# More load buffers for the experts, and another order of the last sums and the last norm, in a fused three-layer block on one core

## The chip, the cores and the metric

The program runs on one core of a Trainium2 chip. The metric is the device time of one execution in microseconds (us); a kernel's time is the median of several runs. Five engines work side by side, each on its own queue in order: TensorE (PE in the profile; its weight loads are PEld), VectorE (DVE), ScalarE (ACT), GpSimd (POOL, unused here) and SyncE (SP), which issues all the DMAs.

## The reference

A first block (three kinds of attention and a SwiGLU) is followed by a second one of two layers; each layer has a mixer and a feed-forward part, each closed by a layer norm. Sequence 256, width 1024, all in float32. The change concerns the last part only, the mixture of experts of the last layer and the layer norm behind it:

```python
def moe_swiglu(h, w_router, w_gate, w_up, w_down):          # 8 experts, 2 per token, width 3584 each
    hf = h.reshape(t, d)
    logits = (hf @ w_router).astype(jnp.float32)
    top_val, top_idx = lax.top_k(logits, TOP_K)
    gates = jax.nn.softmax(top_val, axis=-1)
    ...
    def expert_block(args):
        xb, e = args
        return (jax.nn.silu(xb @ w_gate[e]) * (xb @ w_up[e])) @ w_down[e]
    ...
    out = jnp.einsum('tk,tkd->td', gates.astype(y.dtype), y)

h = layer_norm(DEEPNORM_ALPHA * h + y, ln_g[layer, 1], ln_b[layer, 1])   # eps 1e-5; this is the output
```

## The kernel before

All weights come from DRAM as one stream of tiles of 128 x 2048 float32 (1 MB each), in an order fixed at build time: 142 tiles for what stands ahead of the experts and 42 for each of the eight experts, 478 in all. The class `Stream` keeps that order. It has a first-in, first-out list `free` of buffers ("slots"), and `fill` issues the next load on SP whenever a slot is on the list and the tile's address is known (`base`). SP's queue is in order too: a load whose slot is still being read holds back the loads behind it.

A tile is used in one of two ways. For most matmuls it is first split: ScalarE copies it to a rounded high part `wh` (L307), VectorE subtracts to get the low part `wl` (L309), in two pieces each; `mm3` (L482 to L491) then runs three matmuls for each product, first all that use `wh`, then those that use `wl`. `begin` gives the slot back to `free` behind the split. The parts lie in two rings of four buffers each in the pool `wp` (`HI` and `LO`), and `get` keeps as many tiles split ahead as the ring is long. Or a tile is used whole, in float32 (`get_whole`), and its slot is free when TensorE has read it.

In the experts the slots are two of `wp` (`RAW`), three of `wx`, three of `wx2`, one of `wx3` and one of `wln`, ten together. Besides, `spare`, a tile of the pool `act` under the tag `xl` (two buffers), is lent for one load (`W.lend`, L1707). When that load has been split, the buffer goes to `yy`, the scaled output of a heavy expert; the tag's other buffer holds `macc`, the sum over the experts.

The experts are ordered by how many tokens they got. Experts 0, 2, 4, 6 in this order are "heavy" (`expert`, 128 slots, split weights), 1, 3, 5, 7 are "light" (`expert_few`, 64 slots, whole weights). Each goes through steps c: matmuls of gate and up (`gu`), Silu (ACT) times up (`sg`, DVE), transposes (`uT`), the copy of their result (`uf` or `uh`, ACT), and the matmuls with the down weights (`dn`) of the step before. `turns` deals out steps of heavy and light experts in turn, by hand; in bursts of mostly six tiles. The whole section `experts` is issued in program order on all engines (`manual_schedule(engines=ALL)`). The routing (`gates`, `in_order`) runs inside step 1 of the first heavy expert; `in_order` ends with SP reading the addresses of the experts 1 to 7 (L1367). In step 3 `begin_few` gathers the inputs of all light experts (`few` by DVE, `gx` by PE, `xfew` by ACT).

An expert's output is scaled by its gate (L1486 for a heavy one, `ye` L1622 for a light one) and scattered back to the tokens by matmuls into PSUM (`scatter`, tiles `sp`), and DVE adds that to `macc` (L1456). The scatter of an expert is run later, within a following step (the list `late`). The last light expert does it in another way: in its step 7, ahead of the `dn` matmuls, `macc` is put into four PSUM banks by matmuls with the identity (`sum`, L1611), the scatter adds to these banks, DVE takes statistics from them (L1630) and ACT copies them back to `macc` (L1631).

Then `normed` does the layer norm: mean and variance (L1686), the root by `inv_sqrt` on DVE alone (a first guess by integer shifts and three Newton steps, between them the four subtractions `centred`, L1690, which read `macc`), the four scalings (L1697), and a DMA of each result to the output. Behind it stands `If(most > 0)`: the function `again`, for tokens beyond an expert's room, which runs only if an expert overflowed, and `normed` once more.

Of the kernel before, what the change touches and what calls it, by code (L numbers as in the profile page):

```python
# [216 lines left out]
class Stream:  # L217
# [3 lines left out]
    def __init__(self, nc, src, items, raw, hi, lo):  # L221
# [4 lines left out]
        self.slots, self.free, self.holds, self.count = [], [], {}, {}  # L226
# [10 lines left out]
    def room(self, pools):  # L237

        new = []
        for p in pools:  # L240
            k = self.count[p] = self.count.get(p, 0) + 1
            new.append((p, f"wr{k}"))
        self.slots += new
        self.free = new + self.free

    def _part(self, kind):
        ring = self.rings[kind]
        p = ring[self.turn[kind] % len(ring)]
        self.turn[kind] += 1
        return p.tile([128, 2048], F32R, tag="w" + kind, name="w" + kind, bufs=ring.count(p))  # L250
# [18 lines left out]

    def spare(self):  # L270

        p, tag = self.free.pop(0)
        return p.tile([128, 2048], F32, tag=tag, name="wr", bufs=1)

    def load(self, n):

        while self.n_load < n:
# [4 lines left out]
            self._load(slot[0].tile([128, 2048], F32, tag=slot[1], name="wr", bufs=1))  # L282
# [6 lines left out]
    def lend(self, t):  # L289

        self._load(t)

    def _taken(self, i):
        if i in self.home:
            self.free.append(self.home.pop(i))
# [55 lines left out]
def tile_kernel(ctx: ExitStack, tc: tile.TileContext, cst, par, wst, x, mem, g_mix, g_mem, g_ffn, w_forget,  # L351
# [87 lines left out]

    def inv_sqrt(m, eps, between):  # L440


        v, r, w = (mo.tile([128, 2], F32, name=n) for n in ("iv", "ir", "iw"))
        i = mo.tile([128, 2], I32, name="ii")
        V.tensor_scalar(out=v, in0=m, scalar1=eps, scalar2=None, op0=ALU.add)
        V.tensor_scalar(out=i, in0=v.bitcast(I32), scalar1=1, scalar2=None, op0=ALU.logical_shift_right)
        V.tensor_scalar(out=i, in0=i, scalar1=-1.0, scalar2=float(0x5f3759df), op0=ALU.mult, op1=ALU.add)
        r0 = i.bitcast(F32)
        for step in range(4):
            between[step]()  # L450
            if step == 3:
                return r
            V.tensor_tensor(w, r0, r0, op=ALU.mult)
            V.scalar_tensor_tensor(out=w, in0=w, scalar=-0.5, in1=v, op0=ALU.mult, op1=ALU.mult)
            V.scalar_tensor_tensor(out=r, in0=w, scalar=1.5, in1=r0, op0=ALU.add, op1=ALU.mult)
            r0 = r
# [930 lines left out]
    def hidden(pg, pu):  # L1387

        sg = sm.tile([128, 512], F32, name="sg", tag="sq", bufs=2)[:, 0:pg.shape[-1]]
        A.activation(out=sg, in_=pg, func=AF.Silu)  # L1390
        V.tensor_tensor(sg, sg, pu, op=ALU.mult)
# [40 lines left out]
    spare = act.tile([128, 2048], F32, name="wr", tag="xl")  # L1432
    macc = act.tile([128, 2, D], F32, name="macc", tag="xl")
    yy = act.tile([128, 2, D], F32R, name="yy", tag="xl")
# [25 lines left out]
    def expert(Pm, s, after, late, begun=None, last=False):  # L1460
# [20 lines left out]
        y = (yy[:, 0], yy[:, 1])  # L1481
# [8 lines left out]
        def scatter(t):  # L1490
            for n in range(2):
# [4 lines left out]
                added(t, n, ps, last)  # L1496

        ws = widths(s)
        for c in range(len(ws) + 1):
# [29 lines left out]
            if c == 4 and after is not None:  # L1529
                Pn = slots(rkp[:, :, after], 0)  # L1530
            if c:
# [36 lines left out]
    def expert_few(s, late, last=False):  # L1568
# [15 lines left out]
        for c in range(8):  # L1584
            end = c == 7
            if not end:
# [12 lines left out]
                turn = hidden(ps[:, 0], ps[:, 1])  # L1599
# [6 lines left out]
            if end and last:  # L1606

                for t in range(2):
                    for n in range(2):
                        summed.append(pa("sum"))  # L1610
# [13 lines left out]
        def scatter(t):  # L1624
# [12 lines left out]
    left = {}  # L1637
# [45 lines left out]
    def normed():  # L1683
# [3 lines left out]

        def centred(t, c):
            cc = slice(c * 512, c * 512 + 512)
            return lambda: V.scalar_tensor_tensor(out=done[:, t, cc], in0=macc[:, t, cc], scalar=mv[:, t, 0:1],  # L1690
                                                  in1=gbf[:, cc], op0=ALU.subtract, op1=ALU.mult)

        r = inv_sqrt(mv[:, :, 1], 1e-5, [centred(t, c) for t in range(2) for c in range(2)])
# [78 lines left out]
```

## Time and profile before

| what | us |
|---|---|
| median of 3 runs (1851.49 to 1852.97) | 1852.12 |
| the profiled execution | 1851.57 |
| its span, first to last instruction | 1849.3 |
| TensorE busy (share of the span) | 1809.3 (98%) |
| VectorE busy | 1107.7 (60%) |
| ScalarE busy | 874.0 (47%) |

The profile is one execution; the span leaves out 2.3 us before the first and behind the last instruction. Shares of busy time are means over stages with different limits; matmuls are pipelined and their ends modelled, so a busy TensorE need not be at its peak. "Idle before" an instruction is what its engine stood still, and the name behind the arrow is what ended it. The DMA share is the mean busy share of the core's 16 DMA engines; it can read slightly above 1.

### The profile page before, as it was taken

How to read it: one execution, taken by the hardware profiler on the slowest of the kernel's cores; microseconds unless marked ns; L12 is line 12 of the kernel's file. 1: busy time of each engine (PE TensorE's matmuls, PEld its weight loads, DVE VectorE, ACT ScalarE, POOL GpSimd, SP SyncE). 2: the span in 40 equal slices, each digit the busy share in tenths (PEclk: the TensorE clock that was granted, in tenths of full speed). 3: DMA queues.
4: the chain of work that ended last, by engine and by line, in shares of the span. 5: the costliest groups of instructions: out<-in, count | busy, mean ns of one | idle time of the engine just before them, and what ended most of it. 6: DMA issues, size and time to landing. Idle time of an engine off the chain costs nothing.

```text
span 1849.3 us, 27608 instructions
## 1 busy us (share of the span) xinstructions
PE 1809.3 (98%) x11150; PEld 1443.3 (78%) x11150; DVE 1107.7 (60%) x1609; ACT 874.0 (47%) x1224; POOL 0.2 (0%) x4
## 2 busy tenths in 40 slices
PE   8999999999999999999999999999999999999996
PEld 7888898999899899987787767766777676766662
DVE  7756556554577765467779654664656554654522
ACT  6655565444433354435546444553444444553520
POOL 0000000000000000000000000000000000000000
PEclk9999999999999999999999999999999999999998
DMA  7534344655443555544356799999999999999995
GB/s 263 180 117 157 115 160 171 221 189 203 146 159 135 201 198 195 200 165 159 117 227 237 285 389 420 419 419 420 419 419 419 419 419 420 419 419 419 410 419 220
DMA packets 73287, 512.70 MB, mean 277 GB/s; under 512 B 8512, under 2 KB 9152, under 8 KB 12096
## 3 DMA queue, kind: packets, MB, share of 16 engines
q1 hardware_dynamic: 73152, 510.86, 69.9%
q8 instruction: 89, 1.46, 0.3%
q14 instruction: 46, 0.38, 0.1%
HBM read 509.78 MB, written 1.05 MB: 276 GB/s over the span
## 4 chain that ended last, share of the span: by engine, by line
PE 83%; DMA 9%; DVE 6%; ACT 1%; issue 1%; SPq 0%; DVEq 0%; ACTq 0%
DMA wr<-in_wst_dram 8%; PE gu L1593 8%; PE fm L482 7%; PE fm L493 7%; PE fm L486 7%; PE gu L482 5%; PE gu L484 5%; PE gu L491 5%; PE dn L1617 4%; DVE wl L309 3%; PE tk L482 3%; PE tk L484 3%; PE acc L484 3%; PE tk L491 3%; PE acc L482 3%; PE acc L491 3%
## 5 line engine op out<-in xcount | busy, mean ns | idle before, releaser
L309 DVE TENSOR_TENSOR wl<-wr,wh 128x1024 fp32r<-128x1024 f32 x620 | 729.7, 1219 | 355.4 <-ACT wh L307 340.5
L307 ACT ACTIVATE wh<-wr 128x1024 fp32r<-128x1024 f32 x620 | 617.6, 1051 | 297.6 <-issue 84.4
L482 PE MATMUL fm<-xh,wh 128*128 128x256 f32 x1056 | 251.2, 280 | 0.0
L486 PE MATMUL fm<-xl,wh 128*128 128x256 f32 x1056 | 249.4, 278 | 0.0
L1593 PE MATMUL gu<-wr,xfew 128*64 128x256 f32 x1792 | 207.9, 385 | 0.0
L482 PEld LDWEIGHTS fm<-xh,wh 128*128 128x128 f32 x1056 | 198.8, 188 | 1.1 <-issue 0.2
L486 PEld LDWEIGHTS fm<-xl,wh 128*128 128x128 f32 x1056 | 198.6, 188 | 0.9
L1593 PEld LDWEIGHTS gu<-wr,xfew 128*64 128x64 f32 x1792 | 124.8, 138 | 77.4 <-issue 21.1
L482 PE MATMUL gu<-wh,xe 128*128 128x512 f32 (+1 forms) x448 | 177.7, 398 | 0.0
L484 PE MATMUL gu<-wh,xe 128*128 128x512 f32 (+1 forms) x448 | 173.0, 388 | 0.0
L493 PE MATMUL fm<-xh,wl 128*128 128x256 f32 x1056 | 145.4, 278 | 0.0
L493 PEld LDWEIGHTS fm<-xh,wl 128*128 128x128 f32 x1056 | 131.5, 188 | 0.0
L491 PE MATMUL gu<-wl,xe 128*128 128x512 f32 (+1 forms) x448 | 119.3, 388 | 0.4 <-DVE wl L309 0.4
L482 PE MATMUL tk<-wh,xh 128*128 128x512 f32 x288 | 116.6, 405 | 1.7 <-ACT wh L307 1.5
L484 PE MATMUL tk<-wh,xl 128*128 128x512 f32 x288 | 114.5, 397 | 0.4 <-DVE xl L464 0.4
L482 PEld LDWEIGHTS gu<-wh,xe 128*128 128x128 f32 x448 | 84.2, 188 | 31.6 <-ACT wh L307 13.0
L1581 ACT ACTIVATE uf<-uT 128x256 f32<-128x256 f32 x28 | 10.8, 384 | 204.6 <-PE uT L1579 204.6
L1617 PE MATMUL dn<-wr,uf 128*64 128x512 f32 x448 | 103.1, 594 | 2.8 <-ACT uf L1581 1.4
L491 PEld LDWEIGHTS gu<-wl,xe 128*128 128x128 f32 x448 | 83.0, 188 | 19.0 <-DVE wl L309 1.1
L484 PEld LDWEIGHTS gu<-wh,xe 128*128 128x128 f32 x448 | 84.2, 188 | 16.5 <-DVE xe L464 0.3
L482 PE MATMUL dn<-wh,uh 128*128 128x512 f32 x224 | 89.2, 398 | 0.0
L484 PE MATMUL dn<-wh,ul 128*128 128x512 f32 x224 | 88.0, 393 | 0.0
(348 smaller groups left out, 2281.9 us busy)
## 6 DMA issues: line engine op xcount, KB each, us to landing
wr<-in_wst_dram SPq DMA_DIRECT2D x477, 1024.0 KB, 11.8
gb<-in_ln_g_dram SPq DMA_DIRECT2D x3, 512.0 KB, 5.7
gb<-in_ln_b_dram SPq DMA_DIRECT2D x3, 512.0 KB, 6.5
memt<-in_mem_dram SPq DMA_DIRECT2D x2, 512.0 KB, 6.9
res<-in_x_dram SPq DMA_DIRECT2D x2, 512.0 KB, 12.7
wr<-in_wst_dram SPq DMA_DIRECT2D x4, 256.0 KB, 15.6
out_dram<-wr SPq DMA_DIRECT2D x4, 256.0 KB, 3.1
gb<-in_g_mem_dram SPq DMA_DIRECT2D x1, 512.0 KB, 5.3
```

The source lines that it names most:

```text
L307: self.nc.scalar.activation(out=h[:, c], in_=t[:, c], func=AF.Copy)
L309: return [lambda c=c: self.nc.vector.tensor_tensor(l[:, c], t[:, c], h[:, c].bitcast(F32), op=ALU.subtract) for c in cols]
L482: T.matmul(ps, ah, bh, start=first and i == 0, stop=False)
L484: T.matmul(ps, al, bh, start=False, stop=False)
L486: T.matmul(ps, ah, bl, start=False, stop=False)
L491: T.matmul(ps, ah, bl, start=False, stop=last and i == n - 1)
L493: T.matmul(ps, al, bh, start=False, stop=last and i == n - 1)
L1581: A.activation(out=U, in_=pT, func=AF.Copy)
L1593: T.matmul(ps[h, g], xfew[:, u + k, i * FEW:i * FEW + FEW], w[:, k, 256 * b:256 * b + 256], start=u + k == 0, stop=u + k == KD - 1)
L1617: T.matmul(acc[h], U[:, j, b * FEW:b * FEW + FEW], wd[n][:, k], start=c == 1 and k == 0, stop=end and k == 3)
```

## The change

1. **Slots.** `spare`'s buffer is no longer lent for one load but put at the head of `free` for good. `fewer_parts`, called as the experts begin, shortens each ring of parts from four to three and appends one slot of the tag `wh` and one of `wl` to `free`; the tags keep four buffers each, which parts and loads then share.
2. **`yy`** has no buffer of its own any more. In the last step but one of a heavy expert `keep` marks that the next slot that comes free is held back; in its last step `borrow` makes `yy` in it, and `give`, behind the second scatter's matmuls, puts the slot on `free`.
3. **The last sums.** The identity matmuls of `sum` move from step 7 to step 6 of the last light expert, ahead of that step's `dn`; one of the four banks comes from the other PSUM pool. `normed` reads the sums from PSUM; the copies to `macc` come behind it.
4. **The last root.** `inv_sqrt` is replaced by Ln and Exp on ScalarE with one Newton step on DVE behind the subtractions. Behind the last Silu ScalarE loads the table with Ln and Exp.

```diff
+    def fewer_parts(self):
+        for kind in "hl":
+            ring = self.rings[kind]
+            self.free.append((ring[0], "w" + kind, len(ring)))
+            self.deep[kind] = len(ring)
+            ring.pop()
...
-        return p.tile([128, 2048], F32R, tag="w" + kind, name="w" + kind, bufs=ring.count(p))
+        return p.tile([128, 2048], F32R, tag="w" + kind, name="w" + kind, bufs=self.deep.get(kind, ring.count(p)))
...
+    def keep(self):
+        self.wanted = True
+
+    def borrow(self, name):
+        slot, self.kept = self.kept, None
+        return self._new(slot, F32R, name), lambda: self.free.append(slot)
...
     def _taken(self, i):
         if i in self.home:
-            self.free.append(self.home.pop(i))
+            slot = self.home.pop(i)
+            if self.wanted:
+                self.wanted, self.kept = False, slot
+            else:
+                self.free.append(slot)
...
-    def hidden(pg, pu):
+    def hidden(pg, pu, final=False):
...
         A.activation(out=sg, in_=pg, func=AF.Silu)
+        if final:
+            A.preload_act_table_set(LOGEXP)
...
-    spare = act.tile([128, 2048], F32, name="wr", tag="xl")
     macc = act.tile([128, 2, D], F32, name="macc", tag="xl")
-    yy = act.tile([128, 2, D], F32R, name="yy", tag="xl")
...
-        y = (yy[:, 0], yy[:, 1])
+        y = give = None
...
                 added(t, n, ps, last)
+            if t:
+                give()
...
+            if c == len(ws) - 1:
+                W.keep()
+            if end:
+                yy, give = W.borrow("yy")
+                y = (yy[:, 0:D], yy[:, D:2 * D])
...
-            if end and last:
+            if c == 6 and last:
                 for t in range(2):
                     for n in range(2):
-                        summed.append(pa("sum"))
+                        summed.append((pb if t + n == 0 else pa)("sum"))
                         T.matmul(summed[-1], ident, macc[:, t, n * 512:n * 512 + 512], start=True, stop=False)
...
                 if last:
                     V.bn_stats(out=fst[:, t, n], in_=pss[n])
-                    A.activation(out=macc[:, t, n * 512:n * 512 + 512], in_=pss[n], func=AF.Copy)
+                    sums.append(pss[n])
...
         W.after = True
+        W.fewer_parts()
...
+        V.tensor_scalar(out=v, in0=mv[:, :, 1], scalar1=1e-5, scalar2=None, op0=ALU.add)
+        A.activation(out=r, in_=v, func=AF.Ln)
+        A.activation(out=r, in_=r, func=AF.Exp, scale=-0.5)
+        cols = [(t, slice(n * 512, n * 512 + 512), part(t, n)) for t in range(2) for n in range(2)]
+        for t, cc, ps in cols:
+            V.scalar_tensor_tensor(out=done[:, t, cc], in0=ps, scalar=mv[:, t, 0:1], in1=gbf[:, cc], op0=ALU.subtract,
+                                   op1=ALU.mult)
+        V.tensor_tensor(w, r, r, op=ALU.mult)
+        V.scalar_tensor_tensor(out=w, in0=w, scalar=-0.5, in1=v, op0=ALU.mult, op1=ALU.mult)
+        V.scalar_tensor_tensor(out=r, in0=w, scalar=1.5, in1=r, op0=ALU.add, op1=ALU.mult)
...
-        W.lend(spare)
+        W.free.insert(0, (act, "xl", 2))
...
-        normed()
+        normed(lambda t, n: sums[2 * t + n])
+        for i, ps in enumerate(sums):
+            A.activation(out=macc[:, i // 2, i % 2 * 512:i % 2 * 512 + 512], in_=ps, func=AF.Copy)
```

## Rows read from the trace of the kernel before

**Rows 1.** The page: busy us by engine; DMA share in 40 slices; issues of loads.
```profile
PE 1809.3 (98%) x11150; PEld 1443.3 (78%) x11150; DVE 1107.7 (60%) x1609; ACT 874.0 (47%) x1224; POOL 0.2 (0%) x4
...
DMA  7534344655443555544356799999999999999995
...
wr<-in_wst_dram SPq DMA_DIRECT2D x477, 1024.0 KB, 11.8
```
**Rows 2.** Waits of TensorE from 1062 us on: us in total, times, longest us.
```profile
PE sp L1627 <- DVE macc L1456: 3.1, 2, 2.2
PE dn L1617 <- ACT uf L1581: 1.4, 3, 0.5
PE dn L1617 <- DMA wr<-in_wst_dram: 1.4, 1, 1.4
```
**Rows 3.** Windows: us, busy by engine (PE, PEld, DVE, ACT, POOL), PEclk, DMA share, GB/s.
```profile
995.00:1005.00 10.00, 7.47 (x33) 5.38 (x32) 9.55 (x32) 7.18 (x8) 0.00 (x0) 1.00 0.06 8
1035.00:1045.00 10.00, 10.00 (x50) 8.58 (x50) 3.68 (x5) 6.13 (x9) 0.00 (x0) 1.00 0.23 96
1060.00:1070.00 10.00, 10.00 (x80) 6.82 (x80) 0.00 (x0) 0.16 (x1) 0.00 (x0) 1.00 0.40 138
1070.00:1820.00 750.00, 742.85 (x4277) 516.43 (x4272) 402.77 (x416) 338.07 (x414) 0.00 (x0) 1.00 1.01 419
```
**Rows 4.** Waits of SP, 960 to 1110 us, the largest.
```profile
SPq L266 <- DVE wl L309: 72.8, 28, 12.2
```
**Rows 5.** Timeline near 1685 us: start, us, engine, line, out<-in, count, [idle before, releaser].
```profile
1682.80 2.36 DVE L309 TENSOR_TENSOR wl<-wr,wh 128x1024 fp32r<-128x1024 f32 x2 [13.25 <-ACT wh L307]
...
1685.08 1.27 DVE L1456 TENSOR_TENSOR macc<-macc,sp 128x512 f32<-128x512 f32 x2
1685.81 2.67 PE L1627 MATMUL sp<-ye,PU 64*128 64x512 f32 x4 [2.19 <-DVE macc L1456]
```
**Rows 6.** Window of the stretch at half clock.
```profile
1685.86:1692.68 6.82, 6.82 (x24) 3.36 (x26) 6.82 (x8) 4.35 (x5) 0.00 (x0) 0.50 1.02 420
```
**Rows 7.** Waits of TensorE in the first heavy expert, 985 to 1062 us.
```profile
PE uT L1474 <- DVE sg L1391: 2.1, 1, 2.1
PE gx L1564 <- DVE few L1557: 1.9, 1, 1.9
```
**Rows 8.** Timeline of a heavy burst: fifth and sixth tile split; fourth, fifth used.
```profile
1727.38 4.63 DVE L309 TENSOR_TENSOR wl<-wr,wh 128x1024 fp32r<-128x1024 f32 x4 [0.25 <-ACT wh L307]
...
1732.93 1.08 PE L491 MATMUL gu<-wl,xe 128*128 128x512 f32 x4
...
1735.69 1.09 PE L491 MATMUL dn<-wl,uh 128*128 128x512 f32 x4
```
**Rows 9.** Timeline of TensorE in steps 6 and 7 of the last light expert.
```profile
1817.84 1.04 PE L1617 MATMUL dn<-wr,uf 128*64 128x512 f32 x2
1820.25 3.65 PE L1617 MATMUL dn<-wr,uf 128*64 128x512 f32 x14 [1.37 <-DMA wr<-in_wst_dram]
...
1824.10 3.60 PE L1611 MATMUL sum<-macc,cs 128*128 128x512 f32 x8
1827.63 3.65 PE L1617 MATMUL dn<-wr,uf 128*64 128x512 f32 x16
```
**Rows 10.** Timeline of DVE in the last norm.
```profile
1836.02 0.17 DVE L445 TENSOR_SCALAR iv<-mv 128x2 f32<-128x2 f32 x1
...
1840.26 0.16 DVE L455 SCALAR_TENSOR_TENSOR ir<-iw,ir 128x2 f32<-128x2 f32 x1
...
1841.00 2.73 DVE L1697 SCALAR_TENSOR_TENSOR wr<-wr,ir 128x512 f32<-128x512 f32 x4
```
**Rows 11.** Groups of DVE by line, 950 to 970 us: busy us, mean ns, idle before.
```profile
L977 DVE SCALAR_TENSOR_TENSOR res<-res,nw,gb 128x512 f32<-128x512 f32 x4 | 2.8, 748 | 0.1
...
L966 DVE SCALAR_TENSOR_TENSOR res<-res,acc 128x512 f32<-128x512 f32 x4 | 2.7, 680 | 1.0 <-PE acc L491 1.0
```
**Rows 12.** Timeline of ScalarE in an earlier norm: Ln; Exp takes the same.
```profile
966.32 0.20 ACT L428 ACTIVATE nr<-nv 128x1 f32<-128x1 f32 x1
```

More of the change, by code (lines that the diff above doesn't have):

```diff
@@ L225, in __init__ @@
         self.base = {None: 0}
-        self.slots, self.free, self.holds, self.count = [], [], {}, {}
+        self.free, self.count, self.deep, self.wanted, self.kept = [], {}, {}, False, None
         self.rings = {"h": list(hi), "l": list(lo)}
@@ L241, in room @@
             k = self.count[p] = self.count.get(p, 0) + 1
-            new.append((p, f"wr{k}"))
-        self.slots += new
+            new.append((p, f"wr{k}", 1))
         self.free = new + self.free
+    def fewer_parts(self):
[4 more added lines that the diff above has]
+            ring.pop()
     def _part(self, kind):
@@ L268, in _load, with _new @@
         self.n_load += 1
+    def _new(self, slot, dtype=F32, name="wr"):
+        p, tag, bufs = slot
+        return p.tile([128, 2048], dtype, tag=tag, name=name, bufs=bufs)
     def spare(self):
-        p, tag = self.free.pop(0)
-        return p.tile([128, 2048], F32, tag=tag, name="wr", bufs=1)
+        return self._new(self.free.pop(0))
+    def keep(self):
[3 more added lines that the diff above has]
+        return self._new(slot, F32R, name), lambda: self.free.append(slot)
     def load(self, n):
@@ L281, in load @@
             self.home[self.n_load] = slot
-            self._load(slot[0].tile([128, 2048], F32, tag=slot[1], name="wr", bufs=1))
+            self._load(self._new(slot))
     def fill(self):
@@ L287, in fill @@
             self.load(self.n_load + 1)
-    def lend(self, t):
-        self._load(t)
     def _taken(self, i):
         if i in self.home:
-            self.free.append(self.home.pop(i))
+            slot = self.home.pop(i)
[3 more added lines that the diff above has]
+                self.free.append(slot)
     def begin(self):
@@ L438, in rstd_end @@
         return w
[L440 to L456, printed above, removed]
     def urgent():
@@ L1598, in expert_few @@
                             late.pop(0)()
-                turn = hidden(ps[:, 0], ps[:, 1])
+                turn = hidden(ps[:, 0], ps[:, 1], last and c == 6)
             else:
@@ L1635, in expert_few @@
         return [lambda: scatter(0), lambda: scatter(1)]
-    left = {}
+    left, sums = {}, []
     def heavies(Pm, begun):
@@ L1681, in tile_kernel, with normed @@
     mv = mo.tile([128, 2, 2], F32, name="mv")
-    def normed():
+    def normed(part):
         for t in range(2):
             V.bn_aggr(out=mv[:, t], in_=fst[:, t])
[L1688 to L1693, printed above, removed]
-        for t in range(2):
-            for c in range(2):
-                cc = slice(c * 512, c * 512 + 512)
-                V.scalar_tensor_tensor(out=done[:, t, cc], in0=done[:, t, cc], scalar=r[:, t:t + 1], in1=bbf[:, cc],
-                                       op0=ALU.mult, op1=ALU.add)
-                nc.sync.dma_start(out=out[t * 128:t * 128 + 128, cc], in_=done[:, t, cc])
+        v, r, w = (mo.tile([128, 2], F32, name=n, tag=n) for n in ("iv", "ir", "iw"))
+        V.tensor_scalar(out=v, in0=mv[:, :, 1], scalar1=1e-5, scalar2=None, op0=ALU.add)
[8 more added lines that the diff above has]
+        V.scalar_tensor_tensor(out=r, in0=w, scalar=1.5, in1=r, op0=ALU.add, op1=ALU.mult)
+        for t, cc, ps in cols:
+            V.scalar_tensor_tensor(out=done[:, t, cc], in0=done[:, t, cc], scalar=r[:, t:t + 1], in1=bbf[:, cc],
+                                   op0=ALU.mult, op1=ALU.add)
+            nc.sync.dma_start(out=out[t * 128:t * 128 + 128, cc], in_=done[:, t, cc])
     with tc.manual_schedule(engines=MS):
@@ L1737, in tile_kernel @@
         with tc.manual_schedule(engines=MS):
-            normed()
+            normed(lambda t, n: macc[:, t, n * 512:n * 512 + 512])
 def arrange(inputs):
```

## Prediction

> **What bounds the kernel now.** I read the page first [rows 1]: TensorE is busy 98% of the span, and the DMA engines are at 9 tenths or more over the last 15 slices. So there are two candidates from about 1070 us on, where the weights of the eight experts stream in, and busy shares can't decide between them, since ends of matmuls are modelled. The waits decide: from 1062 us to the end TensorE stood idle for 3.1 us before the second scatter of a light expert (DVE was late with the sum), 1.4 us three times in all for `uf`, which belongs to the last step of each light expert, and 1.4 us for one load, the last but two [rows 2]. Over nearly 790 us that is little: TensorE is the bound and the loads are only just in time. One load is 1024 KB [rows 1]; at the 419 GB/s of the full stream [rows 3] that is 2.50 us. The DMA engines were not always full, though: of the 10 us from 995 they used 0.06, from 1035 0.23, from 1060 0.40 [rows 3], so 23 of 30 us were free, because SP stood in its queue waiting for a buffer: 72.8 us of its waits from 960 to 1110 end with a split by DVE [rows 4]. From 1070 on the share is 1.01, so every load behind that point lands at a fixed place in the stream, and a load started earlier before it moves all of them.
>
> The place where lateness costs is seen near 1680 us [rows 5]. DVE's split of a heavy tile starts at 1682.80, when its load has landed and ScalarE has done its part; the sum of a light expert is queued behind it on DVE and starts at 1685.08; TensorE waits 2.19 us for that sum, to get the PSUM bank. [...]
>
> **The change, part by part.**
>
> *Three buffers.* Slots for whole loads before: 2 in `wp`, 3 in `wx`, 3 in `wx2`, 1 each in `wx3` and `wln`, 10, and `spare` for a single load. After: the same 10, `spare`'s buffer for good, and one out of each ring of parts, 13; `spare`'s one load existed before, so its gain is that the buffer comes back. Three loads are 3 x 2.50 = 7.5 us of stream, and the 23 us that were free before 1070 [rows 3] hold them. So from 1070 on each load lands 7.5 us sooner, and nothing in that needs TensorE to be faster. What this is worth is only what TensorE waited because of loads: 3.1 us at the scatters, and the 3.4 us of half clock behind the longer of these waits, if it follows from it [rows 2, 5, 6]. By then TensorE has gained a few us and the loads 7.5, more than the 2.19 us of lateness. I take both: 6.5 us. Bounds: 0 for the clock if a half-speed stretch stays or turns up elsewhere, 0 for the waits if DVE is late for another reason.
>
> *The rings of parts go from 4 to 3.* ScalarE's copy of a heavy tile now waits for the matmuls of the tile three before it, not four; queued behind it on ScalarE are `uh`, Silu and `uf`, behind DVE's half the sums. In a burst of six heavy tiles the fifth is split on DVE from 1727.38, done 2.3 us later (half of 4.63, two tiles), about 1729.7; TensorE wants that low part at 1735.7 at the latest, and tiles follow at 2.75 us [rows 8]. The lead is some 5.7 us, and one buffer less makes it 3.0: still covered, cost 0. In the first expert it moves one split on DVE (2.36 us, like the pair in [rows 5]) from ahead of `gates` and `in_order` to behind them. TensorE waits there 2.1 us for `sg` and 1.9 us for `few`, both on DVE [rows 7]; DVE reaches these with the same number of splits behind `in_order` as before, and starts that row earlier. I take 1.5 us of gain, nearer to one of the two waits than to both; bounds -1.5 (the split is then needed at once) to +4.0.
>
> *The borrowed `yy`.* From step 6 of a heavy expert to its second scatter 12 slots work, not 13. ScalarE's first write to it waits for the split that emptied the slot, which lies a step back; the next load in that slot waits on SP for the scatter's matmuls, and is put in the queue only behind them. Two loads of lead remain, 5.0 us, over the 2.19 us that was missing: cost 0, bound one load, 2.5 us, in one place.
>
> *The sums.* Before, TensorE runs step 6's `dn` from 1817.84, is held by its load until 1820.25, ends at 1823.9, does the transposes, then the eight matmuls of `sum` from 1824.10, then step 7's `dn` from 1827.63 for 3.65 [rows 9]: 13.4 us from 1817.84. After, `sum` (3.53 from start to the next start) goes ahead of step 6's `dn`. With loads 7.5 us sooner that `dn` needs no wait: 3.53 + 3.65, transposes 0.2, then the 0.47 wait for `uf` (a third of 1.4 [rows 2]), which `sum` covered until now, then 3.65: 11.5. Gain 1.9. It isn't the whole 3.5, because the work is moved and not removed. Check against the loads: 1817.84 less 8.0 (6.5 and 1.5) and plus 3.53 is 1813.4, and the load of 1820.25 lands at 1812.7; the last pieces, two loads or 5.0 us later, at 1817.7, when step 7 starts at 1817.7. So both limits nearly meet here, and more speed upstream would hardly be cashed.
>
> *The norm.* From `iv` at 1836.02 to the first scaling at 1841.00 are 4.98 us on DVE [rows 10]. After: `iv` 0.2, four subtractions, one step of three small operations of 0.16 each [rows 10], with the gaps between them some 0.6 (an estimate from these rows). Ln and Exp take 0.20 each on ScalarE [rows 12] and lie beside the subtractions; without that cover they would cost some 0.7 with their handovers. The subtractions now read PSUM: the like operation took 680 ns from PSUM and 748 from SBUF [rows 11]. 0.2 + 4 x 0.68 + 0.6 = 3.5, gain 1.5; with 748 it is 1.2. ScalarE's four copies come behind the subtractions and end within the landing of the outputs; the table load behind the last Silu has only `uf` behind it, which waits for TensorE's `dn` and transposes: both 0.
>
> [...]
>
> **Sum.** 6.5 + 1.5 + 1.9 + 1.5 = 11.4 us. The profiled execution took 1851.57 (span 1849.3), so 1840.2 for it; the median of the runs is 0.55 higher: **1840.7**.
>
> **The rivals.** *Half the gain:* the half clock stays, or a wait of DVE's queue does: 3.4 to 6.5 less, 1844.1 to 1847.2. For it: stretches at half clock are few and their place isn't in the kernel's hands; DVE's order is unchanged. Against it: the one here follows the longest wait. *Buffers without effect:* SP is held by something other than slots, the loads land as before; then only the end gains, the load of 1820.25 is covered by `sum`: 1.9 and 1.5, 1848.7. Against it: SP's waits are for splits [rows 4]. *Slower, by the shared ring:* loads and parts now share the four buffers of `wh` and of `wl`. If a part is given the buffer that a load held, ScalarE's copy waits for that load's reader, which may be a light expert's matmul further on. The lead of 3.0 us bears one more tile (2.75); with two it is short by 2.5 us in each of the 24 bursts of heavy tiles behind the first light tiles: 60 us, so 1901. It decides from more than one tile. Against it: a buffer goes to whoever asks when it is free, and parts and loads are asked for in turn.
>
> **How the numbers follow.** Forecast 0.55, half the gain 0.25, no effect of buffers 0.08, slower 0.08, and 0.04 for more than 4 us beyond the forecast. The forecast's own low end: the loads allow 0.7 more, the first expert 2.5 more, which moves the loads too, the norm 0.3: 1837.2; its high end is 1844. Range 1836.5 to 1848, which takes in the first two cases. A measurement of this kernel can tell about 0.2%, 3.7 us: faster 0.84, within 0.08 (the buffers without effect), slower 0.08.
>
> **What would show it.** Right: three more loads issued before 1065 us and no stretch without DMA at 1035 to 1045; each later load 7 to 9 us sooner; no wait of TensorE for the scatter's sum; clock 1.0 from 1060 until after the last scatter; `sum` ahead of step 6's `dn` and no wait for its load; 3.5 us from `iv` to the first scaling. Wrong: ScalarE's copies waiting for TensorE in bursts with TensorE waiting for them (ring of three), SP waiting for a buffer of `wh` while others are free, or TensorE still held at the scatters although loads land sooner.

## The result and the profile after

The changed kernel takes **1868.45 us** (median of four runs, 1864.99 to 1871.71), the one before 1851.80: ratio 1.0089, 95% interval 1.0069 to 1.0108. The forecast was 1840.7, the range 1836.5 to 1848. It is slower by 16.7 us where I expected it faster by 11.4. The profiled execution took 1869.42 us, its span is 1867.6.

The page after: busy us by engine, the DMA share in 40 slices, the issues of loads [against rows 1].

```profile
PE 1831.9 (98%) x11150; PEld 1456.3 (78%) x11150; DVE 1106.5 (59%) x1601; ACT 873.2 (47%) x1227; POOL 0.2 (0%) x4
...
DMA  7434344555443455554366699999999999999994
...
wr<-in_wst_dram SPq DMA_DIRECT2D x477, 1024.0 KB, 10.9
```

TensorE does the same 11150 matmuls and is busy 22.6 us longer: the loss is not idle time. Waits of TensorE from 960 us to the end, with the largest first:

```profile
PE dn L492 <- DVE wl L328: 3.8, 2, 3.4
PE gx L1572 <- DVE few L1565: 3.0, 1, 3.0
PE dn L1625 <- ACT uf L1589: 2.0, 4, 0.5
```

The wait at the scatters (3.1 us) and that for a load near the end (1.4) [rows 2] are gone, as forecast; but a slower TensorE alone takes the first of them away too (e2 below), so this is no proof for the buffers yet. In the first heavy expert the waits for `sg` and `few` [rows 7] have given way to longer ones, 3.8 for a low part and 3.0 for `few`, and each runs into a stretch at half clock, which begins 1.5 and 0.7 us before the wait ends (the columns of this view are us, busy of PE, PEld, DVE, ACT, POOL, granted clock, DMA share, GB/s):

```profile
1013.25:1020.07 6.82, 5.01 (x11) 3.64 (x12) 6.79 (x9) 3.09 (x4) 0.00 (x0) 0.50 0.24 67
...
1050.79:1057.62 6.83, 6.13 (x15) 4.91 (x16) 0.89 (x3) 0.60 (x1) 0.00 (x0) 0.50 0.59 247
```

In return the one at 1685 us [rows 6] is gone. Split by split (DVE's split of the same tile, changed against before), the changed kernel is 0.6 to 2 us late near 200 us of the span, 4.7 at 350, 8 to 10 at 520 to 670, 13.2 at 850, 13.9 at 952 and 22.6 at 1072. So some 14 us are lost ahead of the experts, where the instructions and their order are those of before, and some 9 in the first expert. From there on TensorE falls back further, by its starts: 26.1 us late at the last `dn` of the third light expert (1701.39 against 1675.31), and then gains, to 20.0 at the last sums (1852.14 against 1832.10). What the first part looks like, in one window of 150 us with TensorE alone in view, first before, then after (us, busy, matmuls, clock, DMA share, GB/s):

```profile
320.00:470.00 150.00, 150.00 (x1103) 1.00 0.56 204
```

```profile
320.00:470.00 150.00, 150.00 (x1086) 1.00 0.57 203
```

Busy throughout and at full clock in both, but 17 matmuls fewer. Each matmul takes longer.

### The profile page after: what moved, and what is told of

Same layout as the page of the kernel before. It is cut to its first block, busy times and chain, and to the rows that moved or that the text cites. A ratio compares the mean times of both kernels' runs of the same rounds, so it can differ in the third digit from the quotient of the medians.

```text
span 1867.6 us, 27625 instructions
## 1 busy us (share of the span) xinstructions
PE 1831.9 (98%) x11150; PEld 1456.3 (78%) x11150; DVE 1106.5 (59%) x1601; ACT 873.2 (47%) x1227; POOL 0.2 (0%) x4
## 4 chain that ended last, share of the span: by engine, by line
PE 92%; DVE 5%; ACT 1%; issue 1%; DMA 1%; SPq 0%; DVEq 0%; ACTq 0%
PE gu L1601 10%; PE fm L483 7%; PE fm L494 7%; PE fm L487 7%; PE gu L483 6%; PE gu L485 6%; PE gu L492 6%; PE dn L1625 5%; PE acc L485 3%; PE acc L483 3%; PE acc L492 3%; PE tk L485 3%; PE tk L483 3%; PE tk L492 3%; PE dn L492 3%; PE dn L483 3%
## 5 line engine op out<-in xcount | busy, mean ns | idle before, releaser
L483 PE MATMUL fm<-xh,wh 128*128 128x256 f32 x1056 | 257.7, 282 | 0.0
L487 PE MATMUL fm<-xl,wh 128*128 128x256 f32 x1056 | 255.9, 281 | 0.0
L1601 PEld LDWEIGHTS gu<-wr,xfew 128*64 128x64 f32 x1792 | 123.9, 137 | 75.5 <-issue 11.4
L494 PE MATMUL fm<-xh,wl 128*128 128x256 f32 x1056 | 149.2, 281 | 0.0
```

The costliest lines, as they stand in the source:

```text
L483: T.matmul(ps, ah, bh, start=first and i == 0, stop=False)
L487: T.matmul(ps, ah, bl, start=False, stop=False)
L494: T.matmul(ps, al, bh, start=False, stop=last and i == n - 1)
L1601: T.matmul(ps[h, g], xfew[:, u + k, i * FEW:i * FEW + FEW], w[:, k, 256 * b:256 * b + 256], start=u + k == 0, stop=u + k == KD - 1)
```

## The experiments

The table gives the medians; "before" is the kernel before on the same chip in the same set of runs.

| kernel | us | before | ratio, 95% interval |
|---|---|---|---|
| changed | 1868.45 | 1851.80 | 1.0089, 1.0069 to 1.0108 |
| e1: changed, old addresses | 1848.22 | 1851.99 | 0.9981, 0.9971 to 0.9990 |
| e2: before, shifted by 32 bytes | 1867.66 | 1851.99 | 1.0088, 1.0071 to 1.0106 |
| e3: e1, rings shortened later | 1841.84 | 1851.99 | 0.9949, 0.9932 to 0.9965 |
| e4: the new end alone | 1848.17 | 1851.99 | 0.9976, 0.9967 to 0.9986 |
| e5: e3 with two slots, own `yy` | 1842.31 | 1851.44 | 0.9952, 0.9935 to 0.9968 |
| e6: rings behind the routing | 1842.27 | 1851.44 | 0.9951, 0.9934 to 0.9967 |
| e7: ring of three, no slots from it | 1846.28 | 1851.44 | 0.9975, 0.9965 to 0.9985 |
| e8: e3 shifted by 64 bytes | 1859.25 | 1852.71 | 1.0031, 1.0018 to 1.0043 |

### Why each matmul takes longer

The diff removes `inv_sqrt` and with it the integer tile `ii` of the pool `mo`. It held 32 bytes in each partition, and the pool `act` and nearly all that is allocated behind it lies 32 bytes lower in the changed kernel; the rings in `wp` lie ahead of it and stay. The first two experiments move the addresses back, or move them alone.

**e1**, an unused tile in the place of the old one:

```diff
         v, r, w = (mo.tile([128, 2], F32, name=n, tag=n) for n in ("iv", "ir", "iw"))
+        mo.tile([128, 2], I32, name="ii", tag="ii")
```

> The changed kernel with one unused 32-byte tile in the small pool, in the place of the integer tile of the old root. Without it every buffer behind that pool lies 32 bytes lower than in the kernel before; with it all lie where they lay. The instructions are those of the changed kernel. In the traces the changed kernel loses some 13 us between 200 and 850 us of the span, where its instructions and their order are those of before: the pitch of the 128x512 matmuls is 232 instead of 229 ns, of the 128x256 ones 117 to 118 instead of 113 to 114. Theory A, the addresses make the matmuls slower: the pitch goes back to 229 and 114 and the time falls by 13 us up to the experts and some 5 in them, to about 1850. Theory B, the pitch belongs to the chip or to the run and not to the kernel: this kernel behaves like the one before on the same chip up to 900 us, and so does the changed one when it runs there; the time would be about 1868 less what the chip gives. Theory C, something else in the program (its code, its queues) makes the matmuls slower: the pitch stays at 232 and 118 and the time at 1865 to 1872.

**e2**, the kernel before, with the same instructions:

```diff
-        i = mo.tile([128, 2], I32, name="ii")
+        i = r.bitcast(I32)
```

> The kernel before with one edit: the integer tile of the root shares the bytes of the tile of the root, so that all buffers behind the small pool lie 32 bytes lower, as in the changed kernel. Instructions and their order are those of before. Theory A (addresses): pitch of 232 and 118 ns, and 18 us more, about 1870. Theories B and C: 1852, pitch 229 to 230 and 114.

Theory A held in both directions: 20.2 us less with the tile than in the changed kernel, 15.7 more without it than in the one before. The window from 320 to 470 us, in e1 and then in e2:

```profile
320.00:470.00 150.00, 150.00 (x1103) 1.00 0.56 203
```

```profile
320.00:470.00 150.00, 150.00 (x1085) 1.00 0.56 203
```

The number of matmuls goes with the address, not with the kernel. Below is the mean time from the start of a matmul to the next start, in ns, worked out from all records of a group (those over 25 ns from the median left out). "Distance" is the address of the stationary operand less that of the moving one, modulo 256 bytes; no trace holds addresses, so it is worked out from the sizes of the tiles in the two small pools, rounded up to 32 bytes each.

| group, columns, count | distance before, changed | before | e1 | changed | e2 |
|---|---|---|---|---|---|
| `fm` from `xh`, `wh`; 256; 1056 | 64, 96 | 114.5 | 114.5 | 117.9 | 117.9 |
| `gu` from `wh`, `xe`; 512; 864 | 192, 160 | 229.2 | 229.2 | 233.3 | 233.3 |
| `tk` from `wh`, `xh`; 512; 288 | 192, 160 | 230.0 | 230.1 | 233.5 | 233.5 |
| `dn` from `wh`, `uh`; 512; 224 | 64, 64 | 230.8 | 230.7 | 230.5 | 230.6 |

The last row is the control: there neither operand moved, and the pitch didn't either. The matmul next to it in the same step takes the same weights with `ul`, which did move, and it goes from 230.0 ns in e1 to 233.1 in the changed kernel, and from 230.0 in the kernel before to 232.9 in e2. From e1 to the changed kernel the three groups of `fm` (3168 matmuls, 3.5 ns), those of `gu` with `xe` (1296, 3.9) and of `tk` (864, 3.3) come to 11.1 + 5.0 + 2.9 = 19 us. The other groups with a moved operand add 4.8, so the pitches account for all of the 20.2, and for rather more than the 21.8 by which the spans of the two profiled executions differ. That e2 lost less than 20.2 fits its trace: with a slower TensorE the loads are in time, and the wait at the scatters (3.1 us before) and the 6.8 us at half clock behind it are gone.

**m1** measures the matmuls by themselves, for 512 and 256 columns, with the stationary operand moved in 16 steps (`N_OFF`) of 8 elements (`STEP`), 32 bytes each, and the moving one by none or one:

```python
        for turn in range(2):
            for size in (512, 256):
                for m in range(2):
                    for s in range(N_OFF):
                        for n in range(12):
                            k = n % 4
                            T.matmul(ps[turn][:, 0:size], sta[:, s * STEP + k * 128:s * STEP + k * 128 + 128],
                                     mov[:, m * STEP + k * 512:m * STEP + k * 512 + size], start=True, stop=True)
```

> A kernel of its own that computes nothing of the reference: on an otherwise idle core, float32r matmuls of 512 and of 256 columns with their moving operand at two offsets (0 and 32 bytes) and their stationary one at 16 offsets of 32 bytes each, twelve matmuls in a row for each pair, all of it twice. In the kernels 32 bytes between the two operands went with 229.2 against 233.3 ns (512 columns) and 114.5 against 117.9 (256). Theory: what decides is the distance of the two operands modulo some power of two, and it needs no other engine: the pitch of a row of twelve depends on the difference of the offsets alone, the same for both moving offsets once they are subtracted, with steps of 3 to 4 ns; odd multiples of 32 bytes are the slow ones. Rival 1: the address of one operand alone decides, then the pitch goes with the stationary offset whatever the moving one. Rival 2: it is a collision with the traffic of ScalarE, VectorE and the loads, then all rows here have one pitch within 0.5 ns.

Windows of twelve matmuls of 512 columns each, at the distances 0, 96, 160 and 192:

```profile
146.33:149.07 2.74, 2.74 (x14) 1.00 0.00 0
...
154.66:157.46 2.80, 2.80 (x13) 1.00 0.00 0
...
160.25:163.05 2.80, 2.80 (x13) 1.00 0.00 0
163.05:165.81 2.76, 2.76 (x13) 1.00 0.00 0
```

By single starts (the first of each row left out), from 0 in steps of 32 bytes: 226.7, 233.1, 233.3, 234.0, 231.6, 233.7, 229.2, 233.2 ns, then the same again from 256 on, and the same for the moving operand at 32 bytes once the distance is counted; only two of the four rows at distance 0 are slower, 227.7 and 228.9. So on an idle core the distance of the two operands modulo 256 bytes decides, and 192 and 160 give the kernels' own 229.2 and 233.5: the theory, and neither rival. It isn't the odd multiples of 32 alone; 64 is slow too (233.3). The 7.3 ns between 226.7 and 234.0 show that the pitch depends on the addresses, with no other engine at work; what inside TensorE or the memory makes it so, no run here shows.

For 256 columns m1 gave 117.8 ns at 64 and 117.3 at 96, not the 114.5 and 117.9 of the kernels. **m2** and **m3** repeat that in the kernels' order (each chunk of a high part with two moving tiles, then the low part), with four and with eight chunks in a weight tile.

> A kernel of its own that computes nothing of the reference, for the 256-column matmuls. In the first one the pitch of 512 columns followed the distance of the operands modulo 256 bytes as in the kernels (192: 229.2 ns, 160: 233.7), but rows of twelve like matmuls of 256 columns gave 117.7 at a distance of 64 and 117.3 at 96, where the kernels show 114.5 and 117.9. Here the order is the kernels' own: each stationary chunk of the high part is used twice, with a high and a low moving operand, then the low part once; the stationary tiles at 16 offsets of 32 bytes, all of it twice. Theory: in this order the distance decides as well, 114.5 at 64 and 117.9 at 96, period 256. Rival: it stays at 117 to 118 for both; then the 256-column matmuls of the kernels are slowed by something else that goes with the shift (where ScalarE or the loads write), and that stays open.

> A kernel of its own, as the last one, for 256 columns, but with the layout that most of these matmuls have in the kernels: eight chunks in a weight tile, so that both operands move on by 1024 bytes from chunk to chunk, summed up in PSUM. In the kernels this layout went at 113 or at 118 ns, by whole stretches, at a distance of 64 bytes, and always at 117 to 120 at 96; with four chunks it was 116.3 and 119.8. In the second turn four small bf16 matmuls stand ahead of each group of 24. Theory: 113 to 114 at 64 and 117 to 118 at 96, in at least one of the turns. Rival: 117 to 118 at both, as with four chunks on the idle core; then these two operands alone don't explain the 256-column matmuls, and the kernels' 113 needs something that is not in here.

The rival came true in both: 117.7 to 118.0 ns at 64 and 117.3 to 117.4 at 96, 116.8 to 120.1 over all distances (in m3 96 went to 118.8 with the small matmuls between the groups). Two windows of m3, 48 matmuls each, at 64 and at 96 bytes:

```profile
71.68:77.33 5.65, 5.65 (x50) 1.00 0.02 3
77.33:82.97 5.64, 5.64 (x51) 1.00 0.00 0
```

So what I can't reproduce is the fast value. In the kernel before, `fm` runs at 113.6 ns from 320 to 470 us and at 117.8 from 250 to 300, at the same distance, and near 530 us it changes from one group of matmuls to the next: 117.8 at 527.9 us, 113.8 at 532.8, 117.8 at 537.5. Of its 3168 matmuls with `xh` or `xl` 2371 are followed by the next within 114 ns, in the changed kernel none. That it goes with the distance in the kernels is shown (e1, e2, e8); what chooses between 113 and 118 at 64 stays open. Distances of more than 512 bytes were not varied.

**e8** asks whether a distance of 0, the best for 512 columns, is a better place for the whole kernel:

```diff
-        mo.tile([128, 2], I32, name="ii", tag="ii")
+        mo.tile([128, 24], I32, name="ii", tag="ii")
```

> The kernel with the rings shortened later (1841.8 us), all buffers behind the small pool 64 bytes higher, so that stationary and moving operands lie a multiple of 256 bytes apart. On the idle core 512 columns went at 226.6 to 227.7 ns at this distance, and at 229.2 at the distance that the kernel has now (192). Some 3200 of its 512-column matmuls have the shifted operand: 2 ns each, 6.4 us less. For the 256-column ones the idle core gave 118.9 to 119.6 at distance 0 and 117.8 at 64, while the kernel has 114.5 at 64. Theory A: the distance acts on both as on the idle core: 6.4 less and, with 119 for 114.5 in 3400 matmuls, 15 more: 1850. Theory B: 256 columns keep their 114.5: 1835.4.

1859.25, some 17 us over e3 (from another set of runs): theory A in direction, and more than it said, by 9 us. In the profiled executions 3.4 of the 17.5 between the spans are 6.83 us at half clock at 987 us, which e3 doesn't have. Its window:

```profile
320.00:470.00 150.00, 150.00 (x1075) 1.00 0.56 203
```

`fm` went from 114.5 to 119.8 ns, just what the idle core shows at 0 (119.5); 3168 times 5.3 is 16.8, more than the 15 of theory A. `gu` with `xe` came down by 0.4 to 1.5 ns only, not by 2. So the old place was a good one for `fm`, by accident.

### Why the first expert lost

**e3**, from e1:

```diff
-        W.fewer_parts()
...
         for i, who in enumerate(order):
             next(both[who])
+            if i == 2:
+                W.fewer_parts()
```

> The changed kernel with the buffers at the addresses of before, and with the rings of parts shortened behind step 3 of the first expert instead of ahead of the experts. The slots of the two rings so come some 50 us later. Theory: the splits that stand ahead of the gates and of the routing are what TensorE waited for at 1014.7 and 1051.5 us of the changed kernel's span (4.5 and 3.2 us instead of 2.9 and 2.0 before), and each of these waits was followed by a stretch of 6.8 us at half clock, 3.4 us lost. So this one is 8 to 10 us faster than the kernel that differs from it in this alone, and DVE's splits stand ahead of the gates again. Rival: the waits are longer because the loads are, and stay; then within 2 us of it.

6.4 us faster than e1, between theory and rival and nearer to the theory, and with **1841.84** the fastest kernel here. The 8 to 10 of the theory were taken from the changed kernel, with 6.8 us at half clock behind each of two waits; in e1 the second such stretch is 3.4. TensorE's waits in e1, then in e3:

```profile
PE dn L492 <- DVE wl L328: 4.1, 2, 3.6
PE gx L1572 <- DVE few L1565: 3.1, 1, 3.1
```

```profile
PE uT L1475 <- DVE sg L1394: 2.6, 2, 2.1
...
PE gx L1572 <- DVE few L1565: 1.9, 1, 1.9
```

What makes the first of them is seen best in the changed kernel: DVE's timeline near the gates and TensorE's at the wait (start, us, engine, line, out<-in, count, [idle before, releaser]):

```profile
1002.91 2.36 DVE L328 TENSOR_TENSOR wl<-wr,wh 128x1024 fp32r<-128x1024 f32 x2 [0.52 <-DMA wr<-in_wst_dram]
1005.18 0.15 DVE L1444 TENSOR_TENSOR gt<-m 128x1 f32<-128x1 f32 x1
...
1013.36 0.15 DVE L1367 TENSOR_SCALAR cint<-cmax 128x1 int32<-128x1 f32 x1
1013.44 4.63 DVE L328 TENSOR_TENSOR wl<-wr,wh 128x1024 fp32r<-128x1024 f32 x4
...
1014.72 0.80 PE L492 MATMUL dn<-wl,uh 128*128 128x512 f32 x1 [3.45 <-DVE wl L328]
```

From 1005.18 to 1013.44 DVE is at `gates` and `in_order`. TensorE takes its matmuls with the high part at 1010.19, ends them at 1011.3 and needs the low part, whose split stands behind that row. So TensorE has 6.1 us of work left when the row begins, and DVE needs 8.3 for the row and 1.2 for the first piece of the split: the 3.4 or 3.5 us between are the wait. With the rings still at four (e3) that split stood ahead of the row. TensorE gets a tile of 2.75 us further, waits 0.4 there, and then for `sg`:

```profile
986.67 2.36 DVE L328 TENSOR_TENSOR wl<-wr,wh 128x1024 fp32r<-128x1024 f32 x2 [0.48 <-ACT wh L326]
988.95 0.15 DVE L1444 TENSOR_TENSOR gt<-m 128x1 f32<-128x1 f32 x1
...
997.20 4.63 DVE L328 TENSOR_TENSOR wl<-wr,wh 128x1024 fp32r<-128x1024 f32 x4
...
999.62 0.74 PE L492 MATMUL gu<-wl,xe 128*128 128x512 f32 x2 [0.40 <-DVE wl L328]
1002.49 0.66 PE L1475 MATMUL uT<-cs,sg 128*128 128x128 f32 x4 [2.13 <-DVE sg L1394]
```

The spans of the two profiled executions differ by 5.8 us. By starts 1.7 of it are the first waits (3.7 and 0.9 in e1 against 0.6 and 2.3) and 1.2 the wait for `few` (3.2 against 2.0). The rest is clock. Windows at half clock, e1:

```profile
999.13:1005.96 6.83, 6.27 (x15) 4.72 (x15) 6.83 (x7) 2.01 (x2) 0.00 (x0) 0.50 0.49 185
1036.68:1040.09 3.41, 3.41 (x10) 2.70 (x9) 0.00 (x0) 0.60 (x1) 0.00 (x0) 0.50 0.78 329
```

and e3, where only the second is left:

```profile
1031.38:1034.79 3.41, 3.41 (x10) 2.67 (x9) 0.00 (x0) 0.60 (x1) 0.00 (x0) 0.50 1.02 425
```

TensorE is busy for 9.68 us at half clock in the one and 3.41 in the other; half of the difference is 3.1 us of work. 1.7 + 1.2 + 3.1 = 6.0, so more than half of the loss is clock.

**e6** shortens the rings behind step 1 (`i == 0` in the diff above).

> Addresses as before; the rings are shortened behind step 1 of the first expert, so behind the gates and the routing, but ahead of the inputs of the light experts. Shortened ahead of the experts, TensorE waited 3.7 and 0.9 us there for a low part, then 3.2 us for the inputs of the light experts, at 1848.2 us; shortened behind step 3, 0.6 and 2.3, then 2.0, at 1841.8. Theory: each wait is longer by itself, because one split of VectorE stands behind the small operations instead of ahead of them; here the first is as in the late one and the second as in the early one: 2 to 4 us over the late one, 1844 to 1846. Rival: the second wait only follows from the first; then 1841.8.

1842.27, not above e3 by anything that can be told: the rival. TensorE waits there 2.1 us for `sg` and 1.4 for `few`. So what costs is the one split at `gates` and `in_order`, not the one ahead of `few`. But the second wait doesn't simply follow from the first either, as the next run shows: with the long first wait it is 1.3 us there. What sets the wait for `few`, from 1.3 to 3.1 us, wasn't settled.

**e7** takes the depth of three from the start, but leaves all four buffers to the parts:

```diff
     def fewer_parts(self):
         for kind in "hl":
             ring = self.rings[kind]
-            self.free.append((ring[0], "w" + kind, len(ring)))
             self.deep[kind] = len(ring)
             ring.pop()
```

> Addresses as before; the splits are issued three tiles ahead instead of four from the start of the experts on, as in the changed kernel, but the tags keep their four buffers for parts alone and no load gets one: 11 slots, with the borrowed outputs. Theory: it is the order of issue, not the sharing of buffers, that makes TensorE wait: the same 3.7, 0.9 and 3.2 us with half clock behind as in the changed kernel at the old addresses (1848.2), and less gain from the loads, 1848 to 1854. Rival: the parts wait for buffers that loads hold; then these waits go back to 2.9 and 2.0 us, and 1842 to 1847.

TensorE's waits:

```profile
PE dn L491 <- DVE wl L327: 3.9, 2, 3.5
...
PE sp L1634 <- DVE macc L1456: 1.8, 1, 1.8
PE gx L1571 <- DVE few L1564: 1.3, 1, 1.3
```

The wait for the low part is there, with no load in any of these buffers. It is the order of issue, not the sharing: the theory, for this wait. The time, 1846.28, is lower than the theory said and in the rival's range: I had put both long waits into it, and `few` was waited for only 1.3 us, with no half clock behind it.

### What the gains are worth

**e4** is the kernel before with the hunks of `hidden`, `expert_few` and `normed` alone, at the old addresses.

> The kernel before with only the end changed: the last sums go to PSUM in step 6, the root is ScalarE's, the norm reads PSUM; loads, rings and the outputs' tile are as before, and all buffers lie where they lay. By the steps of the prediction: 1.9 us for the sums and 1.5 for the norm, 1848.4 to 1849; the load that held step 6's matmuls back is then covered by the sums. Rival: the sums are only moved, and the load's wait and the statistics take their place: 1850 to 1852.

1848.17: 3.8 us, with 2.6 to 6.1 by the interval; forecast 3.4.

**e5** is e3 without the borrowed outputs and the third slot:

```diff
+    spare = act.tile([128, 2048], F32, name="wr", tag="xl")
     macc = act.tile([128, 2, D], F32, name="macc", tag="xl")
+    yy = act.tile([128, 2, D], F32R, name="yy", tag="xl")
...
-        y = give = None
+        y = (yy[:, 0], yy[:, 1])
...
-                yy, give = W.borrow("yy")
...
-        W.free.insert(0, (act, "xl", 2))
+        W._load(spare)
```

> Addresses as before, the new end, and the two slots out of the rings (behind step 3 of the first expert); the outputs keep their own buffer and the third slot is left out: 12 slots instead of 13. The kernel with three slots took 1841.8 us, the one with none and the same end 1848.2. In the latter TensorE waits 2.4 us at the one scatter and 0.7 at the other, and half a stretch of 3.4 us follows. Two loads are 5.0 us, more than 2.4. Theory: the whole gain is there already, 1841.5 to 1842.5. Rival: each load counts by itself, two thirds of the gain, 1844.

1842.31 against 1841.84: the whole gain is there with two slots. In order of slots, TensorE's wait at the scatters is 2.6 us in all with ten of them (e4), 1.8 with eleven (e7, above) and gone with twelve (e5) and thirteen. e4's row for it, and then the largest waits of e3 from 1062 us on:

```profile
PE sp L1611 <- DVE macc L1440: 2.6, 2, 2.1
```

```profile
PE dn L1625 <- ACT uf L1589: 2.0, 4, 0.5
PE gx L1416 <- DVE ul L465: 0.9, 1, 0.9
```

The half clock behind that wait goes with it: e4 has it at 1689.6 us and e7 at 1686.9, 3.41 us each, and e3 and e5 have none from 1040 us to the last sums.

## Why the prediction was wrong

| part | forecast, us | measured, us | from |
|---|---|---|---|
| sums and norm | -3.4 | -3.8 | e4 against before |
| three buffers | -6.5 | -6.3, of which 4.3 shown as theirs | e3 against e4 |
| rings of three in the first expert | -1.5 | +6.4 | e1 against e3 |
| addresses | not in the sum | +20.2 | changed against e1 |
| all | -11.4 | +16.5 | |

**The term that was missing** decides. I costed instructions, waits and buffers, and gave the tile `ii` no step, though the diff shows that it goes and `mo` is made just ahead of `act`. So the sum took the shift of the addresses at nothing, without a reason; the runs show 20.2 us for it (changed against e1). No rival covered it either: my slower case was the shared ring, 1901 us. With the addresses of before the change gives 1848.2, faster than before and just outside the range, 7.5 us short of the forecast; that second miss is the rings of parts, below.

**The buffers** gave 6.3 us where 6.5 was forecast, but that they agree so well is partly luck. What the forecast named is there: the waits at the scatters are gone, 2.6 us in e4, and so is the half clock behind them, 3.41 us in e4 and 1.7 of work; together 4.3. Another 3.1 us of the 7.3 between the spans of the two profiled executions are half clock in places that the buffers do not explain. Here are e4's three stretches, the first of them ahead of anything that the change touches; e3 has only the one of 3.41 us at 1031 us:

```profile
40.99:44.40 3.41, 3.41 (x9) 2.68 (x9) 2.92 (x6) 3.29 (x6) 0.00 (x0) 0.50 0.58 240
1003.55:1010.38 6.83, 6.11 (x17) 4.97 (x18) 6.83 (x8) 4.03 (x5) 0.00 (x0) 0.50 0.79 293
1689.63:1693.04 3.41, 3.41 (x20) 1.92 (x17) 3.41 (x5) 2.83 (x3) 0.00 (x0) 0.50 1.02 420
```

The four of e4's ten executions whose mean clock is that of e3's (0.996) took 1846.4 to 1847.9 us, 4.5 to 6.1 more than e3. So the loads are worth something between 4.3 and 6.3, and the term that was too large is the clock behind the scatter: 3.4 of work in the forecast, from 6.82 us at a granted clock of 0.50 in one execution [rows 6], and 1.7 in e4, from 3.41.

Each later load is issued and lands sooner. Load 250 lands at 1247.0 us in e3 and 1254.5 in the kernel before, load 470 at 1799.9 and 1807.6, so 7.5 to 7.7 us, where I said 7 to 9; 2.0 of it are there at load 150 already, ahead of the experts. In e1, with short rings from the start, load 250 lands at 1252.9: what TensorE loses in the first expert holds the loads back too. One mark was wrong for e3: from 1035 to 1045 us its DMA share is 0.10, not higher than before [rows 3] (in e1 it is 0.44); its loads gained their time at 995 (0.28) and from 1060 on (0.79):

```profile
995.00:1005.00 10.00, 7.47 (x33) 5.39 (x32) 9.76 (x22) 7.13 (x9) 0.00 (x0) 1.00 0.28 98
1035.00:1045.00 10.00, 10.00 (x51) 8.56 (x50) 3.86 (x5) 5.96 (x8) 0.00 (x0) 1.00 0.10 27
1060.00:1070.00 10.00, 10.00 (x82) 6.80 (x82) 0.00 (x0) 0.34 (x1) 0.00 (x0) 1.00 0.79 306
```

Three were more than was needed; two do it (e5).

**The rings of parts.** In the bursts the cost was 0, as said: from 1062 us on TensorE waits for no `wl` in any of these traces. In the first expert the step failed. I saw that one split moves behind `gates` and `in_order`, wrote that it may then be needed at once, priced that at 1.5 us, and took a gain instead, because DVE reaches `sg` sooner. TensorE doesn't get to `sg`: it stands at the split two tiles earlier. The row of small operations takes 8.3 us and the first piece of the split 1.2; that sum of 9.5 was the number to set against the 6.1 us of work that a ring of three leaves TensorE there. And I counted no clock behind a wait of 3.5 us, though [rows 5, 6] show 6.82 us at half clock behind a wait of 2.19.

**The borrowed `yy`** cost nothing that can be told (e3 against e5). **The shared ring** as a rival is out: e7 has the wait without sharing, and the bursts have none with it.

**The sums.** e3's timeline of TensorE, to be set against [rows 9]:

```profile
1811.85 3.70 PE L1619 MATMUL sum<-macc,cs 128*128 128x512 f32 x8
1815.48 3.65 PE L1625 MATMUL dn<-wr,uf 128*64 128x512 f32 x16
...
1820.04 3.65 PE L1625 MATMUL dn<-wr,uf 128*64 128x512 f32 x16 [0.53 <-ACT uf L1589]
```

From 1811.85 to the end of the last `dn`, 1823.69, are 11.8 us; it was 13.4, and 11.5 was forecast. No load holds step 6, and the wait for `uf` is open now, as I said: gain 1.6, not 1.9, mostly because transposes and wait take 0.97 us from 1819.07 to 1820.04, where I had 0.2 and 0.47.

**The norm.** DVE in e3 [against rows 10]:

```profile
1828.44 0.17 DVE L1699 TENSOR_SCALAR iv<-mv 128x2 f32<-128x2 f32 x1
1828.52 2.73 DVE L1704 SCALAR_TENSOR_TENSOR wr<-sum,mv,wr 128x512 f32<-128x512 f32 x4
...
1831.74 2.74 DVE L1710 SCALAR_TENSOR_TENSOR wr<-wr,ir 128x512 f32<-128x512 f32 x4
```

3.30 us from `iv` to the first scaling, where it was 4.98 and 3.5 was forecast. The gain comes from the shorter row of small operations, not from PSUM, and there I read [rows 11] wrongly: its two lines are different operations, 680 and 748 ns long. The subtraction itself took the same time from SBUF (748 ns) and from PSUM (746). The groups in the kernel before (`macc`, SBUF) and in e3 (`sum`, PSUM), with the mean ns of one behind the busy us:

```profile
L1690 DVE SCALAR_TENSOR_TENSOR wr<-macc,mv,wr 128x512 f32<-128x512 f32 x4 | 3.0, 748 | 0.4 <-issue 0.4
```

```profile
L1704 DVE SCALAR_TENSOR_TENSOR wr<-sum,mv,wr 128x512 f32<-128x512 f32 x4 | 2.7, 746 | 0.0
```

In both, what follows a subtraction starts 0.66 to 0.67 us after it, as instructions overlap; the four in e3 take 2.64 from 1828.52 to 1831.16.

**Two slips in the working** moved nothing: [rows 1] has 16 slices at 9 tenths and then one at 5, and the lead in [rows 8] is 6.0 us, not 5.7.

## What to carry to other kernels

A diff that adds or drops a tile, however small, moves every buffer allocated behind it; list which matmul operands move against which others, and if TensorE is busy all the time and yet does fewer matmuls in a window, put the old addresses back with an unused tile before anything else is asked. A ring's depth counts against the longest row of work that the engine filling it does in between (9.5 us here with the split, against 6.1 us of work ahead), not against the steady pace of a burst, so shorten it behind that row. More load buffers were worth here what the engine waited for loads and the half clock behind those waits (2.6 and 1.7 us, up to 6.3 in all); two more slots bought all of it. And when a term comes out as forecast, look at the clock of both executions first: stretches at half clock, 3.41 or 6.83 us long (1.7 or 3.4 of work), lay in other places from kernel to kernel: at 1031 us in e3, at 41, 1004 and 1690 in e4, at 987 in e8.

## What the runs showed of the hardware

On an idle core the pitch of float32r matmuls went with the distance of the stationary from the moving operand modulo 256 bytes, varied over 512: 226.7 to 234.0 ns for 512 columns (m1), 117 to 120 for 256 (m1 to m3). In the whole kernel 32 bytes were 16 to 20 us (0.9 to 1.1%; e2 against before, changed against e1), and 64 bytes the other way some 17 (e8 against e3), of which 3.4 can be clock. The distance alone doesn't give every number: `dn` with `uh`, at 64 bytes, takes 230.8 ns in the kernels, where m1 has 233.3, and in the kernels 256 columns run at 113.6 or at 117.8 at one and the same distance.

A wait of TensorE wasn't always followed by half clock (0.50 granted): at the 2.1 us for `sg` it came in e2, e4, e5, e6 and e8, for 3.41 or 6.83 us, and not in the kernel before and in e3. It also came without such a wait: at 839 us in the kernel before (3.41 us), at 973 in e5 and e6 and at 987 in e8 no wait of more than 0.6 us stands within 10 us ahead. Nor did the kernel alone fix it: in the 19 executions of the kernel before in the set of e1 to e4 the mean clock was 0.992 to 0.997. What a wait cost in clock can so be bounded from the rows, by 0 and 3.4 us, but not told ahead.
